# Two casts, two products, a broadcast and a preparation step change places in a two-layer encoder kernel

## The chip, the cores and the metric

The kernel runs on one NeuronCore of a Trainium2 chip. Its time is the device time of one execution in microseconds (us). TensorE (PE in the profile) multiplies matrices, VectorE (DVE), ScalarE (ACT) and GpSimd (POOL) do element work, and SyncE (SP) issues most of the loads. Each engine runs its own queue of instructions in order; an instruction that waits for another engine holds all that stand behind it in its queue.

## The reference

Two sequences, 256 and 512 positions of width 1024, run through the same two layers. A layer is a mixer and a feed-forward part, each behind a normalisation whose scale, shift and gate come from a conditioning vector. Layer 0 mixes with an mLSTM of four heads in both directions, layer 1 with attention in a window of 128 around each position (16 query heads, 4 key heads). Cut to what matters here:

```python
def trunk(x, c, ...):
    for l in range(DEPTH):                                   # 2
        mod = jax.nn.silu(c) @ adaln_w[l] + adaln_b[l]
        sh1, sc1, g1, sh2, sc2, g2 = [...]
        h = rmsnorm(x, norm_g[l, 0]) * (1 + sc1) + sh1
        y = mlstm_mixer(h, ...) if l % N_MIXERS == 0 else swa_mixer(h, ...)
        x = x + g1 * y
        h = rmsnorm(x, norm_g[l, 1]) * (1 + sc2) + sh2
        x = x + g2 * conv_ffn(h, ffn_w_up[l], ffn_conv_w[l], ffn_conv_b[l], ffn_w_down[l])
    return rmsnorm(x, final_g)

def conv_ffn(h, w_up, conv_w, conv_b, w_down):
    u = h @ w_up                                             # 1024 -> 2 * 2816
    u = lax.conv_general_dilated(u, ...) + conv_b            # 3 taps, each channel alone
    g, val = u[..., :D_FF], u[..., D_FF:]
    return (jax.nn.silu(g) * val) @ w_down
```

All is float32.

## The kernel before

The 768 positions lie along the free dimension, the channels on the 128 partitions: `x` is eight blocks (`c` from 0 to 7) of 128 x 768, in slabs of four. A float32 product is made from two rounded parts: ACT casts a weight or a factor to a high part (`whi`, `zh`, `s1h`, L276), DVE subtracts to get the low part (`wlo`, `zl`, `s1l`, L277), and PE adds three matmuls, high by high, low by high and high by low. Weights come in `raw` tiles of 128 x 1024 (512 KB, six buffers, L285), their parts lie in three buffers each.

**Feed-forward.** The up projection is done in 11 parts of 4 channel blocks; a part is two pairs (`i` = 0 and 1), a pair is a two-by-two block product in Strassen's way, with seven products instead of eight. `pair` (L1471) loads two weight tiles, makes sums of their halves (POOL, L1479 to L1491), splits them, and gathers the products in fixed banks of the accumulator memory. L1495 copies rows that are finished into a bank, on which PE then adds (the bank copy); L1500, L1506 and L1519 copy further sums out of or between banks; L1524 and L1525 add two sums into result rows. `s1h` and `s1l` are the parts of one weight sum, for the fifth product. The rows then pass the convolution (`conv`: L1679 on ACT, L1681 and L1682 on DVE, 771 elements), `silu` (L1689, ACT) and `product` (L1695, POOL, gate times value, 128 x 772), whose result is split on ACT and DVE for the down product.

Part 0 of a layer is done otherwise, by `head` (L1550 on): both of its pairs at once, in an order written by hand for PE, ACT and DVE, mixed with the end of the mixer's output projection. `last_tile` is that projection as a generator: each step gives one block's matmuls, and the residual sum L548 on DVE. Behind each block follows its square for the normalisation (L113, ACT) and the sum of squares (L122, DVE), and PE adds the squares up over the partitions (L138). `prepare` makes the weight sums and parts for `head` ahead of time.

**Order elsewhere.** Outside `head`, a scheduler places the instructions from a cost model, and `issue_after` tells it that what follows must not be issued ahead of a named instruction. The code around `pair` uses it to hang `silu` and `product` of an earlier part on two copies (`behind`): L1506 for the gates, L1519 for the split.

**mLSTM.** The heads come one after another. `maxima` broadcasts two rows of running maxima of the next head from memory into a slab (L676, two loads of 384 KB on SP). ACT makes exponentials of them (L768 to L775, tile `E`), from which come the weights `PT`. PE sums `PT` by the values into `pa` banks, ACT scales one bank into the output (L828) and DVE adds the other (L829), which frees the banks.

## Time and profile before

| | |
|---|---|
| median of three runs | 1801.85 us (1797.5 to 1803.8) |
| the profiled execution | 1795.42 us |
| its span | 1793.5 us |
| granted TensorE clock, mean | 0.998 |
| PE, DVE, ACT, POOL busy | 98%, 77%, 50%, 28% |

A profile row of a timeline gives the start in us, the duration, the engine, the line, the operation, and the tiles it writes and reads; in square brackets stands how long the engine idled before it and what released it. Matmuls of 128 x 384 start about 0.17 us apart when nothing is waited for. A row of the waits gives what waited, for what, the sum in us, the count and the longest. A tile's number is left out in the profile and given in the listings of the order below.

### The profile page before, as it was taken

The numbers are of one execution on the slowest core, as the hardware profiler recorded it, in microseconds if no ns is written. First come the engines' busy times: TensorE is split into PE (matmuls) and PEld (weight loads), VectorE is DVE, ScalarE is ACT, GpSimd is POOL, SyncE is SP. The second block draws the span as 40 slices with busy tenths as digits, with TensorE's granted clock in tenths as the row PEclk, the third lists the DMA queues.
The fourth block names the chain that finished last, engine by engine and source line by source line (L and its number), as shares of the span: only waits on it lengthen the run. The fifth ranks groups of instructions, "written<-read, shape, count | busy, mean of one in ns | idle before, by whom it ended". The sixth has DMA issues, their size and how long they took to land.

```text
span 1793.5 us, 28843 instructions
## 1 busy us (share of the span) xinstructions
PE 1763.6 (98%) x11164; PEld 1643.1 (92%) x11164; DVE 1380.5 (77%) x2197; ACT 897.8 (50%) x1806; POOL 506.3 (28%) x425
## 2 busy tenths in 40 slices
PE   9999999999989999999999999999999999999998
PEld 6988888989989999999999998989989999999998
DVE  5797678976897777777778867767897777777777
ACT  4455444543574444444444666664564444444443
POOL 1111011230234333333332123320244333333323
PEclk9999999999999999999999999999999999999999
DMA  9265756554222222222223222142122222222202
GB/s 375 97 196 174 230 199 199 164 181 142 71 71 71 71 68 65 61 66 71 71 71 108 86 80 61 44 146 83 47 71 71 71 71 71 71 71 71 71 24 71
DMA packets 64180, 184.02 MB, mean 103 GB/s; under 512 B 6211, under 2 KB 24291, under 8 KB 63916
## 3 DMA queue, kind: packets, MB, share of 16 engines
q1 hardware_dynamic: 63260, 180.77, 31.5%
q8 instruction: 87, 1.43, 0.3%
q0 software_dynamic: 208, 0.90, 0.1%
q10 hardware_dynamic: 576, 0.52, 0.1%
q14 instruction: 49, 0.40, 0.1%
HBM read 175.73 MB, written 6.44 MB: 102 GB/s over the span
## 4 chain that ended last, share of the span: by engine, by line
PE 87%; DVE 7%; DMA 3%; issue 2%; ACT 2%; SPq 0%; POOL 0%; POOLq 0%; DVEq 0%; ACTq 0%
PE ps L270 27%; PE pa L270 24%; PE ps L1447 11%; PE ps L1448 11%; PE ps L1450 11%; PE pa L1286 1%; DVE junk L488 1%; DMA raw<-in_w_dram 1%; DMA slab<-in_adaln_h_dram 1%; DVE wlo L277 1%; DMA raw<-in_adaln_t_dram 1%; PE pa L1447 1%; PE pa L1448 1%; PE pa L1450 0%; DVE slab L277 0%
## 5 line engine op out<-in xcount | busy, mean ns | idle before, releaser
L276 ACT CAST whi<-raw 128x1024 fp32r<-128x1024 f32 x227 | 238.0, 1050 | 307.8 <-PE pa L270 144.6
L277 DVE TENSOR_TENSOR wlo<-raw,whi 128x1024 fp32r<-128x1024 f32 x227 | 295.0, 1300 | 109.1 <-ACT whi L276 106.7
L270 PE MATMUL pa<-slab,whi 128*128 128x256 f32 (+1 forms) x1280 | 306.9, 335 | 0.0
L270 PEld LDWEIGHTS pa<-slab,whi 128*128 128x128 f32 x1280 | 222.3, 188 | 21.2
L548 DVE SCALAR_TENSOR_TENSOR slab<-pa,mod,slab 128x256 f32<-128x256 f32 (+1 forms) x320 | 188.0, 604 | 67.8 <-PE pa L270 67.7
L270 PE MATMUL pa<-slab,wlo 128*128 128x512 f32 (+1 forms) x640 | 204.7, 333 | 0.0
L270 PE MATMUL ps<-zh,whi 128*128 128x256 f32 (+1 forms) x520 | 179.0, 345 | 0.6 <-ACT whi L276 0.6
L1447 PE MATMUL ps<-zh,whi 128*128 128x384 f32 x504 | 171.5, 340 | 4.8 <-ACT ps L1495 2.4
L270 PE MATMUL ps<-zl,whi 128*128 128x256 f32 (+1 forms) x520 | 174.7, 336 | 0.9 <-DVE zl L513 0.8
L270 PE MATMUL ps<-zh,wlo 128*128 128x256 f32 (+1 forms) x520 | 173.4, 335 | 0.2 <-DVE wlo L277 0.2
L270 PE MATMUL ps<-slab,whi 128*128 128x384 f32 (+2 forms) x704 | 172.1, 330 | 0.9 <-DVE slab L277 0.5
L1448 PE MATMUL ps<-zl,whi 128*128 128x384 f32 x504 | 170.1, 337 | 0.8 <-DVE zl L1404 0.8
L1450 PE MATMUL ps<-zh,wlo 128*128 128x384 f32 x504 | 169.0, 335 | 0.0
L488 DVE CUSTOM_DVE_ANT_0 junk<-raw,crow,cstt 128x1024 bf16<-128x1024 f32 x112 | 148.3, 1324 | 11.1 <-DMA raw<-in_adaln_t_dram 10.4
L1695 POOL TENSOR_TENSOR slab<-slab 128x772 f32<-128x772 f32 x44 | 87.0, 1976 | 239.2 <-DVE slab L1682 239.2
L270 PEld LDWEIGHTS pa<-slab,wlo 128*128 128x128 f32 x640 | 120.5, 188 | 13.2
L1681 DVE SCALAR_TENSOR_TENSOR slab<-slab,cstt,slab 128x771 f32<-128x771 f32 x88 | 111.1, 1265 | 26.3 <-ACT slab L1679 26.3
L1479 POOL TENSOR_TENSOR raw<-raw 128x512 f32<-128x512 f32 x40 | 67.3, 1682 | 212.2 <-DMA raw<-in_w_dram 106.0
L270 PEld LDWEIGHTS ps<-slab,whi 128*128 128x128 f32 x704 | 122.3, 188 | 3.4 <-ACT whi L276 0.9
L1682 DVE SCALAR_TENSOR_TENSOR slab<-slab,cstt,slab 128x771 f32<-128x771 f32 x88 | 113.9, 1294 | 0.8
L270 PE MATMUL ps<-slab,wlo 128*128 128x384 f32 (+2 forms) x352 | 114.2, 327 | 0.1
L270 PEld LDWEIGHTS ps<-zh,whi 128*128 128x128 f32 x520 | 98.3, 189 | 17.0 <-issue 6.4
(327 smaller groups left out, 4292.6 us busy)
## 6 DMA issues: line engine op xcount, KB each, us to landing
raw<-in_w_dram SPq DMA_DIRECT2D x206, 512.0 KB, 3.7
raw<-in_adaln_t_dram SPq DMA_DIRECT2D x56, 512.0 KB, 4.2
raw<-in_adaln_w_dram SPq DMA_DIRECT2D x24, 512.0 KB, 4.4
slab<-in_x_dram SPq DMA_DIRECT2D x12, 512.0 KB, 6.9
slab<-in_adaln_h_dram SPq DMA_DIRECT2D x12, 512.0 KB, 9.3
xs<-slab SPq DMA_DIRECT2D x6, 512.0 KB, 3.4
bt<-brow SPq DMA_DIRECT2D x16, 192.0 KB, 3.3
slab<-xs SPq DMA_DIRECT2D x6, 512.0 KB, 6.0
```

The source lines that it names most:

```text
L270: self.nc.tensor.matmul(out, lhsT, rhs, start=start, stop=stop)
L276: nc.scalar.copy(hi, src)
L277: return nc.vector.tensor_tensor(lo, src, hi.bitcast(F32), ALU.subtract)
L488: nc.vector.tensor_tensor_reduce(out=junk, in0=w, in1=row[:, s], scale=1.0, scalar=self.cst(AB + 48 * l + j), op0=ALU.mult, op1=ALU.add, a ...
L548: return self.nc.vector.scalar_tensor_tensor(x, o, self.mod[l][:, gc + c, q : q + 1], x, ALU.mult, ALU.add)
L1447: mm(o, wh[:, k], hi[k], start=start and k == 0, stop=False, skip_group_check=True)
L1448: mm(o, wh[:, k], lo[k], start=False, stop=False, skip_group_check=True)
L1450: mm(o, wl[:, k], hi[k], start=False, stop=k == 3, skip_group_check=True)
L1479: tt(q[2], q[2], q[3], ALU.add)
L1681: stt(y[:, 1:], u[:, :-1], w(0), y[:, 1:], ALU.mult, ALU.add)
L1682: stt(y[:, :-1], u[:, 1:], w(2), y[:, :-1], ALU.mult, ALU.add)
L1695: nc.gpsimd.tensor_tensor(y, y, yrow[:, j], ALU.mult)
```

## The change

Five edits. All products and sums stay; only engine and order change.

1. In `head`, the cast of `top`, the sum of the second pair, into a spare slab, and the two subtractions behind it, move from before the last projection blocks to behind them.
2. In `pair` of part 1, second pair, the convolutions of the first pair's rows are started behind the bank copy and the `s1l` subtraction, by a new argument `start`, and not ahead of the pair.
3. The products of part 0 (those whose split is held back, `wait`) are made by DVE and not by POOL. There are two per layer.
4. `prepare` may issue only behind the square of the second block of the first half's normalisation (`Norm.second`).
5. The maxima of the next head may issue only behind the last weight load that the head before has issued (`last_load`).

```diff
@@ Norm.square
-        net.nc.scalar.activation(sq, self.x(c), AF.Square)
+        act = net.nc.scalar.activation(sq, self.x(c), AF.Square)
         self.sums.append(sq)
         self.count += 1
+        if self.count == 2:
+            self.second = act.ins
@@ raw
-        self.nc.sync.dma_start(t, src)
+        self.last_load = self.nc.sync.dma_start(t, src)
@@ mLSTM
                 soon = self.slab([P, 4, T])
-                maxima(h + 1, soon)
+                with self.tc.issue_after(self.last_load.ins):
+                    maxima(h + 1, soon)
@@ pair
-        self.fp_copy_split(s1h, s1l, q[2])
+        sub = self.fp_copy_split(s1h, s1l, q[2])
...
-        nc.scalar.copy(b, fork)
+        act = nc.scalar.copy(b, fork)
+        if start:
+            with self.tc.issue_after(act.ins), self.tc.issue_after(sub.ins):
+                start()
@@ head
-        nc.scalar.copy(s1[1][0], top)
         wc[0], low = split(ra[0])
         next(last_tile)
         for t in banks[0][1:]:
             mark(t)
         next(last_tile)
-        tt(s1[1][1], top, s1[1][0].bitcast(F32), ALU.subtract)
-        tt(top, a22, q[1][0], ALU.subtract)
         self.norm.add()
+        low()
         next(last_tile)
         self.norm.begin(1)
         next(last_tile)
-        low()
         for _ in last_tile:
             pass
+        nc.scalar.copy(s1[1][0], top)
+        tt(s1[1][1], top, s1[1][0].bitcast(F32), ALU.subtract)
+        tt(top, a22, q[1][0], ALU.subtract)
@@ ffn
-        early = self.prepare(u0, pool)
+        with self.tc.issue_after(self.behind.second):
+            early = self.prepare(u0, pool)
@@ product
-                nc.gpsimd.tensor_tensor(y, y, yrow[:, j], ALU.mult)
+                (nc.vector if wait else nc.gpsimd).tensor_tensor(y, y, yrow[:, j], ALU.mult)
@@ up
-                for j in range(2):
-                    conv(urow[:, 2 * i + j], yrow[:, 2 * i + j], i * FC + 2 * p + j)
+                def convs(i=i):
+                    for j in range(2):
+                        conv(urow[:, 2 * i + j], yrow[:, 2 * i + j], i * FC + 2 * p + j)
+                start = None
+                if p == 1 and i == 0:
+                    start = convs
+                else:
+                    convs()
```

`self.behind` is the normalisation of the first half behind the mixer. The lines of the new text lie two to eight further down: L1495 becomes L1499, L1519 becomes L1526, L1681 and L1682 become L1689 and L1690, L1695 becomes L1703.

The first place is the end of the projection in layer 0, on ACT. `slab_4988` is the spare slab, `nt_4967`, `nt_5024` and `nt_5058` are squares, `whi_4994` is the high part for `wc[0]`. Before:

```order
L113 ACTIVATE nt_4933<-slab_4394 128x384
L113 ACTIVATE nt_4967<-slab_4394 128x384
L1576 CAST slab_4988<-raw_4696 128x512
L1570 CAST whi_4994<-raw_4690 128x1024
L113 ACTIVATE nt_5024<-slab_4394 128x384
L113 ACTIVATE nt_5058<-slab_4394 128x384
L160 ACTIVATE nr_5072<-pa_5053 128x3
```

With the change, for the same stretch:

```order
L113 ACTIVATE nt_4933<-slab_4394 128x384
L1577 CAST whi_4993<-raw_4690 128x1024
L113 ACTIVATE nt_4967<-slab_4394 128x384
L113 ACTIVATE nt_5023<-slab_4394 128x384
L113 ACTIVATE nt_5056<-slab_4394 128x384
L1595 CAST slab_4988<-raw_4696 128x512
L162 ACTIVATE nr_5072<-pa_5051 128x3
```

The cast into the slab now stands behind both last squares, and the cast of `wc[0]` ahead of three of them.

The second place is the second pair of part 1 in layer 0, on DVE. `slab_5409` holds the convolved rows of part 0 and `slab_5423` those of part 1, `slab_5410` the split product of part 0, `s1l_5788` belongs to the next pair. Before:

```order
L1681 SCALAR_TENSOR_TENSOR slab_5409<-slab_4982,cstt,slab_5409 128x771
L1682 SCALAR_TENSOR_TENSOR slab_5409<-slab_4982,cstt,slab_5409 128x771
L277 TENSOR_TENSOR wlo_5542<-raw_5531,whi_5541 128x1024
L1681 SCALAR_TENSOR_TENSOR slab_5409<-slab_4982,cstt,slab_5409 128x771
L1682 SCALAR_TENSOR_TENSOR slab_5409<-slab_4982,cstt,slab_5409 128x771
L1524 TENSOR_TENSOR slab_4983<-ps_4387,nt_5446 128x384
L277 TENSOR_TENSOR wlo_5546<-raw_5529,whi_5545 128x1024
L1525 TENSOR_TENSOR slab_4983<-ps_4386,nt_5489 128x384
L277 TENSOR_TENSOR slab_5410<-slab_5409,slab_5410 128x772
L1681 SCALAR_TENSOR_TENSOR slab_5423<-slab_4983,cstt,slab_5423 128x771
L277 TENSOR_TENSOR s1l_5788<-raw_5776,s1h_5787 128x512
```

With the change:

```order
L1689 SCALAR_TENSOR_TENSOR slab_5409<-slab_4982,cstt,slab_5409 128x771
L1703 TENSOR_TENSOR slab_5409<-slab_5409 128x772
L1690 SCALAR_TENSOR_TENSOR slab_5409<-slab_4982,cstt,slab_5409 128x771
L279 TENSOR_TENSOR wlo_5536<-raw_5525,whi_5535 128x1024
L1689 SCALAR_TENSOR_TENSOR slab_5409<-slab_4982,cstt,slab_5409 128x771
L1531 TENSOR_TENSOR slab_4983<-ps_4387,nt_5446 128x384
L279 TENSOR_TENSOR wlo_5540<-raw_5523,whi_5539 128x1024
L1690 SCALAR_TENSOR_TENSOR slab_5409<-slab_4982,cstt,slab_5409 128x771
L1532 TENSOR_TENSOR slab_4983<-ps_4386,nt_5489 128x384
L279 TENSOR_TENSOR slab_5410<-slab_5409,slab_5410 128x772
L279 TENSOR_TENSOR s1l_5788<-raw_5776,s1h_5787 128x512
L1703 TENSOR_TENSOR slab_5409<-slab_5409 128x772
```

One product (L1703) comes in ahead of `s1l_5788` and one behind it, the convolution of `slab_5423` leaves its place ahead of it, and L1531 stands ahead of a convolution step. On ACT the bank copy now stands ahead of the convolution's own step (L1687), which before stood ahead of it, and the cast `whi_5539` ahead of the second `silu`.

The third place is head 2 of the mLSTM, on ACT. `slab_2807` is the slab of head 3's maxima, `slab_1932` that of head 2, which takes its output. Before:

```order
L823 ACTIVATE dn_2838<-pa_2847 128x1
L828 ACTIVATE slab_1932<-pa_2813,dn_2812 128x256
L831 ACTIVATE nt_2836,ss_2811<-slab_1932 128x256
L828 ACTIVATE slab_1932<-pa_2839,dn_2838 128x256
L831 ACTIVATE nt_2862,ss_2811<-slab_1932 128x256
```

With the change:

```order
L827 ACTIVATE dn_2838<-pa_2847 128x1
L778 ACTIVATE E_3306<-slab_2807,aT 128x384
L832 ACTIVATE slab_1932<-pa_2813,dn_2812 128x256
L774 ACTIVATE E_3306<-E_3306,aT 128x128
L771 ACTIVATE E_3325<-slab_2807,aT 128x128
L778 ACTIVATE E_3325<-slab_2807,aT 128x256
L773 ACTIVATE E_3306<-E_3306,aT 128x128
L835 ACTIVATE nt_2836,ss_2811<-slab_1932 128x256
L832 ACTIVATE slab_1932<-pa_2839,dn_2838 128x256
```

The exponentials of head 3, which stood 19 rows ahead of the first L828, are now mixed with the scaling of head 2's output. On SP the two broadcast loads move from between the weight loads `raw_2562` and `raw_2568` to behind `raw_2803`, past twelve loads.

More of the change, by code (lines that the diff above doesn't have):

```diff
@@ L568, in out_proj @@
         self.norm = norms[1]
+        self.behind = norms[0]
         self.turn = 1
@@ L1469, in outset, with pair @@
         self.evict(r1, o)
-    def pair(self, pool, u, bank, rows, rest=False, behind=None):
+    def pair(self, pool, u, bank, rows, rest=False, behind=None, start=None):
         nc = self.nc
@@ L1719, in up @@
                         bank = lambda j: self.pa()[:, :H] if j == 1 and other else fixed(j)
-                        self.pair(pool, u0 + 3 * p + i, bank, rows, p == 1, held.pop() if held else None)
-                for j in range(2):
-                    conv(urow[:, 2 * i + j], yrow[:, 2 * i + j], i * FC + 2 * p + j)
+                        self.pair(pool, u0 + 3 * p + i, bank, rows, p == 1, held.pop() if held else None, start)
+                def convs(i=i):
+                    for j in range(2):
+                        conv(urow[:, 2 * i + j], yrow[:, 2 * i + j], i * FC + 2 * p + j)
+                start = None
+                if p == 1 and i == 0:
+                    start = convs
+                else:
+                    convs()
                 if i == 0:
```

## The prediction

> **What bounds the kernel now.** I read the page first, then the waits of the TensorE queue, and then the timelines of the engines round the longest of those waits.
>
> ```profile
> span 1793.5 us, 28843 instructions
> PE 1763.6 (98%) x11164; PEld 1643.1 (92%) x11164; DVE 1380.5 (77%) x2197; ACT 897.8 (50%) x1806; POOL 506.3 (28%) x425
> ```
>
> TensorE (PE) is busy for 98% of the span, and no other engine for more than 77%: PE's matmuls, end to end, are the time. The change touches no matmul, so only PE's idle time, about 30 us, can move. The waits say where it is; each row gives the waiting PE group, what released it, the sum, the count and the longest:
>
> ```profile
> PE ps L1450 <- DVE s1l L277: 3.8, 2, 1.9
> PE pa L138 <- DVE nt L122: 3.4, 2, 1.7
> PE ps L1447 <- ACT ps L1495: 2.4, 2, 1.2
> PE ps L1447 <- ACT nt L1519: 2.0, 2, 1.0
> PE pa L1286 <- ACT pt L1290: 1.5, 2, 0.9
> PE pa L270 <- DVE slab L277: 0.2, 1, 0.2
> ```
>
> The four largest waits come twice each, once per layer, and all four (11.6 us) lie in the code that the change rewrites. The order of instructions on PE itself is otherwise kept. So the question is how much of some 13 us each edit frees, and what is late next.
>
> **Edit 1, the early cast in head(), once per layer.** Layer 0, at the end of the projection, in the timelines of ACT, DVE and PE:
>
> ```profile
> 469.81 0.62 ACT L1576 CAST slab<-raw 128x512 fp32r<-128x512 f32 x1 [5.13 <-PE ps L270]
> 471.28 0.52 ACT L113 ACTIVATE nt<-slab 128x384 f32<-128x384 f32 x1
> 466.30 0.62 DVE L548 SCALAR_TENSOR_TENSOR slab<-ps,mod,slab 128x384 f32<-128x384 f32 x1 [1.03 <-PE ps L270]
> 471.83 0.56 DVE L122 TENSOR_TENSOR nt<-nt,nt 128x384 f32<-128x384 f32 x1
> 470.49 0.34 PE L270 MATMUL ps<-slab,wlo 128*128 128x384 f32 x1
> 472.54 0.80 PE L138 MATMUL pa<-inv,nt 128*128 128x2 f32 x6 [1.71 <-DVE nt L122]
> ```
>
> ACT sat 5.13 us on the cast L1576, whose target is a slab that the projection's last tiles still read. Behind it stood the square L113 of a row block that DVE had finished at 466.92. The square ran at 471.28, its sum L122 ended at 472.39, and PE started at 472.54, although its last projection matmul had started at 470.49. Two neighbouring matmuls of this shape start 0.18 apart, so PE lost 2.05 - 0.18 = 1.87 us.
>
> After the change the square stands ahead of that cast and needs only the 466.92. Even behind the cast of wc[0] (1.05, as every ACT cast of 128x1024 whose row is quoted below) it ends by 468.5, and the sum by 469.1, before PE's own 470.66. So this wait goes whole. What is late next is the second half's last square, after the last tile: its residual, square and sum (0.6 + 0.5 + 0.6) follow 470.7, so it is done at about 472.4, when the first sums have run on PE and the next products can cover it. The moved cast and the two subtractions now stand behind the tile loop. They feed only the second pair's fifth product, which PE reaches after four starting products of the layer, and that lead hides them; without it they cost 1.4 (two subtractions of 128x512, 0.68 each as in s1l's row below). I take 1.85 per layer, **3.7**. The bounds per layer are 1.87, and -0.2 if the second sum shows whole (0.65) and the lead is gone (1.4).
>
> **Edits 2 and 3, the second pair of part 1, once per layer.** Three PE waits follow one another here, the last at the fifth product of the next pair. The rows of DVE, POOL and ACT in layer 0:
>
> ```profile
> 517.13 1.22 DVE L277 TENSOR_TENSOR wlo<-raw,whi 128x1024 fp32r<-128x1024 f32 x1
> 518.87 2.06 DVE L1681 SCALAR_TENSOR_TENSOR slab<-slab,cstt,slab 128x771 f32<-128x771 f32 x1
> 520.97 2.51 DVE L1682 SCALAR_TENSOR_TENSOR slab<-slab,cstt,slab 128x771 f32<-128x771 f32 x1
> 523.40 2.32 DVE L277 TENSOR_TENSOR wlo<-raw,whi 128x1024 fp32r<-128x1024 f32 x1
> 525.64 1.01 DVE L1681 SCALAR_TENSOR_TENSOR slab<-slab,cstt,slab 128x771 f32<-128x771 f32 x1
> 526.69 1.02 DVE L1682 SCALAR_TENSOR_TENSOR slab<-slab,cstt,slab 128x771 f32<-128x771 f32 x1
> 527.63 0.55 DVE L1524 TENSOR_TENSOR slab<-ps,nt 128x384 f32<-128x384 f32 x1
> 528.09 2.67 DVE L277 TENSOR_TENSOR wlo<-raw,whi 128x1024 fp32r<-128x1024 f32 x1
> 530.69 0.54 DVE L1525 TENSOR_TENSOR slab<-ps,nt 128x384 f32<-128x384 f32 x1
> 531.16 1.59 DVE L277 TENSOR_TENSOR slab<-slab,slab 128x772 fp32r<-128x772 f32 x1
> 532.67 1.01 DVE L1681 SCALAR_TENSOR_TENSOR slab<-slab,cstt,slab 128x771 f32<-128x771 f32 x1
> 533.60 0.68 DVE L277 TENSOR_TENSOR s1l<-raw,s1h 128x512 fp32r<-128x512 f32 x1
> 534.20 0.95 DVE L277 TENSOR_TENSOR slab<-slab,slab 128x772 fp32r<-128x772 f32 x1
> 517.24 2.88 POOL L1479 TENSOR_TENSOR raw<-raw 128x512 f32<-128x512 f32 x1 [4.10 <-DVE slab L1682]
> 520.08 2.58 POOL L1695 TENSOR_TENSOR slab<-slab 128x772 f32<-128x772 f32 x1
> 522.62 2.02 POOL L1491 TENSOR_TENSOR raw<-raw,raw 128x512 f32<-128x512 f32 x1
> 527.86 1.83 POOL L1695 TENSOR_TENSOR slab<-slab 128x772 f32<-128x772 f32 x1 [3.22 <-DVE slab L1682]
> 529.64 2.28 POOL L1479 TENSOR_TENSOR raw<-raw 128x512 f32<-128x512 f32 x1
> 525.62 0.47 ACT L1519 COPY nt<-ps 128x384 f32<-128x384 f32 x1
> 529.21 0.47 ACT L1495 COPY ps<-slab 128x384 f32<-128x384 f32 x1
> ```
>
> The first wait: the copy L1519 stands behind a weight cast that came late because POOL did a product (L1695, 2.58) ahead of the subtraction L1491. The second: the bank copy L1495 stands behind a convolution on ACT and, through bank 4387, behind DVE's L1524. The third: s1l, done at 534.28, stands at the end of a DVE queue in which whatever overlaps a POOL row is stretched (1.01 to 2.51, 1.22 to 2.67).
>
> Since PE's matmuls do not depend on which wait came when, the gain here is how much earlier s1l ends, up to the 4.1 us that the three waits hold (1.0 + 1.2 + 1.9). From 518.87 to s1l, DVE's unstretched work before is 1.01 + 1.02 + 1.22 + 1.01 + 1.02 + 0.55 + 1.22 + 0.54 + 0.95 + 1.01 + 0.68 = 10.2 us; it took 15.4, so 5.2 us are stretch, beside 10.0 us of POOL rows inside that window (11.59 less the 1.63 before 518.87). After, DVE gains one product (0.95, the nearest row being the 128x772 subtraction of two slabs) and loses the first L1681 of the moved convolutions (1.01): 10.2 again. POOL keeps the tail of L1479 (1.25), L1491 (2.02) and the next L1479 (2.28): 5.6 us, so at the same share 2.9 us of stretch. Then s1l ends at 518.87 + 10.2 + 2.9 = 532.0, which is 2.3 earlier; if POOL's last row comes after s1l (its load is released by a wlo subtraction) it is 1.2 more, 3.5. I take 2.7 per layer, **5.4** for both. The other inputs are in time: the copy L1519 follows a cast that can now start when L1491 ends, near 522.2, and the bank copy follows L1524, near 526.2, with PE due at 527.1. So waits one and two all but go, and about 1.5 to 2 us stay at the third.
>
> [...]
>
> The bounds: the low one has every operation as long as its longest row: 2.06 + 1.59 + 2.51 + 2.67 + 2.06 + 0.55 + 2.67 + 2.51 + 0.54 + 1.59 + 0.68 = 19.4, s1l at 538.3, a loss of 4.0 per layer. The high one is the gain of 4.1.
>
> The convolutions that move behind the bank copy feed part 1's own gates, due a pair later. DVE's second product, behind s1l now, feeds the second half of part 0's down products, which PE takes up only behind the rest of that fifth product and the first half. I cost both at nothing; were that lead gone, it would be one more product, 0.95 per layer.
>
> **Edit 4, prepare() held back.** Only in layer 1 does work move: casts and subtractions for the first Strassen pair leave the attention tail.
>
> ```profile
> 1178.41 1.05 ACT L276 CAST zh<-raw 128x1024 fp32r<-128x1024 f32 x1 [2.33 <-DMA raw<-in_w_dram]
> 1179.37 0.36 ACT L1290 COPY pt<-pa 128x256 f32<-128x256 f32 x1
> 1208.31 0.69 DVE L1546 TENSOR_TENSOR raw<-raw 128x512 f32<-128x512 f32 x1 [1.77 <-DMA raw<-in_w_dram]
> ```
>
> ACT's copy L1290, for which PE waits (1.5 us in two waits above), ran right behind such a cast, which had stood on a load; without it the copy can start up to 0.96 us earlier, more than the longest of the two waits. I take **1.3** of the 1.5, bounds 0 and 1.5. The casts and subtractions land in the output projection; on DVE they are 1.22 + 1.22 + 1.36 = 3.8 us, and DVE idled 1.77 us there ahead of 1208.31. The other 2.0 us are covered by the lead that the weight splits have on PE; without that cover they are the price.
>
> **Edit 5, the maxima.** The two broadcast loads for head 3 move behind the last weight load on SP's queue.
>
> ```profile
> DMA to landing us min/median/max: 4.5/6.8/8.1
> 249.46 2.40 SPq L285 DMA_DIRECT2D raw<-in_w_dram  x2
> 260.65 3.79 PE L270 MATMUL pa<-slab,PT 128*128 128x258 f32 x30
> ```
>
> The gain is the 0.2 us at the last of the waits above, since a weight no longer loads beside them. The price: they are issued at about 251.9 and land near 258.7, at worst 260.0; ACT now reads them ahead of L828, which frees the banks that PE wants at 260.65. At 258.7 plus a 0.6 us exponential it still fits; at 260.0 it costs about 0.5, and 1.0 when the second bank slips too. I take **0.2**, bounds -1.0 and 0.2.
>
> **The sum.** 3.7 + 5.4 + 1.3 + 0.2 = 10.6 us. The span of 1793.5 becomes 1782.9. The profiled execution took 1795.4 against a median of 1801.85 of the runs shown, which differ among themselves from 1797.5 to 1803.8; taken off that median the sum gives 1791.2, and I say **1791**.
>
> **Rivals.** *DVE takes back the pair.* The product goes to the engine that already ends last there (DVE s1l is the largest wait), so s1l could stay at 534.3. Then 3.7 + 1.3 + 0.2 = 5.2 is left: 1796.6. For it speaks DVE's unstretched work, which does not shrink; against it the 5 us of stretch and the POOL rows that leave.
>
> *Slower: the DVE queue overflows.* If the added product waits on POOL as L1682 did, and all behind it as in the low bound, s1l ends 4.0 later per layer: 8.0 - 5.2 = 2.8 us slower, 1804.7. It decides once s1l ends after about 536.9, 2.6 us later than now. Against it: two of POOL's four later rows leave the window.
>
> *Waits only move.* PE reaches the next place early and waits there: the second half's sum after edit 1 and the third wait of edits 2 and 3 take all but a few us, and the output projection pays its 2.0: of the 10.6 us, 5.4 and 1.3 stay away and 2.0 are paid, so 1.9 are gained, 1800.0. For it speaks that ACT and DVE follow PE closely in all these places; against it DVE's idle time right after head's wait.
>
> **Chances.** The forecast 0.64, the first rival 0.18, moved waits 0.11, slower 0.07. A measurement of this kernel tells about 0.3% (5.4 us) from no change, so faster is below 1796.4, slower above 1807.3. The forecast gives 0.64 to faster, and the first rival, which ends beside the bound, half of its own and moved waits a little: 0.75. The rest of these two and a part of the last, whose 2.8 us lie within the bound, are the same: 0.20. That leaves 0.05 for slower. All bounds together run from 1788 (3.7 + 8.2 + 1.5 + 0.2 = 13.6 gained) to 1813 (0.4 + 8.0 + 2.0 + 1.0 = 11.4 lost); they will not all fall on one side. The range reaches over the first rival and most of moved waits, and below 1788 by 2.5 us for the scatter of medians: 1785.5 to 1800.
>
> **What would show it.** Edit 1: no PE wait at L138 above 0.3, ACT's slab cast behind both squares. Edits 2 and 3: the PE waits on the copies L1495 and L1519 (L1499 and L1526 in the new text) under 0.4 each, s1l still a wait of 1.5 to 2, L1703 on DVE at about 1 us. Edit 4: the pt wait under 0.4. Edit 5: no PE wait on slab L832. The prediction is wrong if s1l ends later than before relative to the pair's first matmul, or if new PE waits above 1 us stand in the output projection or at 260.

## The result, and the profile after

The changed kernel takes 1787.5 us, median of four runs (1784.4 to 1788.9), against 1802.4 of the kernel before (1797.5 to 1803.8): a ratio of 0.992, with a 95% interval of 0.9896 to 0.9943. A second comparison, told below, gave 0.9928 (0.9912 to 0.9944). That is faster by more than 0.3%, inside the range, and 3.5 us below the 1791 of the forecast. The profiled execution took 1784.4 us with a span of 1782.3, where the sum had led to 1782.9. Two of the runs below (edits 1 and 3 undone) had one slow execution among ten, 1963 and 4442 us, and their medians and ratios leave it out, as the ratios do for one of the kernel before.

The page's first rows after:

```profile
span 1782.3 us, 28844 instructions
PE 1761.7 (99%) x11164; PEld 1643.4 (92%) x11164; DVE 1377.7 (77%) x2201; ACT 896.2 (50%) x1806; POOL 494.9 (28%) x421
```

PE's idle time fell from 29.9 to 20.6 us, which is 9.3 of the span's 11.2. The waits of the TensorE queue (waiting group, what released it, sum, count, longest) tell where; these are the rows of the changed places and behind them that are left above 0.2 us, and the row of the scaled output, slab L832, that the prediction names:

```profile
PE ps L1454 <- DVE s1l L279: 2.1, 2, 1.6
PE ps L1451 <- ACT ps L1513: 1.4, 2, 0.7
PE pa L272 <- DVE slab L550: 0.8, 1, 0.8
PE pa L272 <- ACT slab L832: 0.4, 1, 0.4
```

Five of the six waits that the prediction started from have no row any more: the norm's sum (3.4), the bank copy (2.4), the copy nt (2.0), pt (1.5) and the weight's low part (0.2). The wait for s1l, the sixth, shrank from 3.8 to 2.1. That for the scaled output, slab L832 (L828 before), is what it was, 0.4; it stands at 179 us, in an earlier head than the one whose loads moved. Two have grown or are new: the copy L1513, at 0.3 in the kernel before (there L1506), and slab L550, which had none at this place.

**The head.** Layer 0 after the change, timelines of ACT, DVE and PE (start, duration, then in brackets the idle time before and what ended it):

```profile
466.05 0.53 ACT L113 ACTIVATE nt<-slab 128x384 f32<-128x384 f32 x1 [3.58 <-DVE slab L550]
470.62 0.53 ACT L113 ACTIVATE nt<-slab 128x384 f32<-128x384 f32 x1 [4.05 <-DVE slab L550]
471.06 0.60 ACT L1595 CAST slab<-raw 128x512 fp32r<-128x512 f32 x1
466.61 0.56 DVE L124 TENSOR_TENSOR nt<-nt,nt 128x384 f32<-128x384 f32 x1 [0.59 <-ACT nt L113]
469.60 0.34 PE L272 MATMUL ps<-slab,wlo 128*128 128x384 f32 x1
469.77 0.72 PE L140 MATMUL pa<-inv,nt 128*128 128x2 f32 x6
471.84 0.72 PE L140 MATMUL pa<-inv,nt 128*128 128x2 f32 x6
```

The square now waits for its row block alone, its sum L124 ends at 467.17, and PE starts the sums at 469.77, 0.17 after its last projection matmul: no gap. The cast that stood ahead of it runs at 471.06, behind both squares, and the second sums at 471.84 have no wait either.

**The pair.** The second pair of part 1 in layer 0, timelines of DVE and POOL:

```profile
516.03 2.06 DVE L1689 SCALAR_TENSOR_TENSOR slab<-slab,cstt,slab 128x771 f32<-128x771 f32 x1
518.01 2.06 DVE L1703 TENSOR_TENSOR slab<-slab 128x772 f32<-128x772 f32 x1
519.99 1.01 DVE L1690 SCALAR_TENSOR_TENSOR slab<-slab,cstt,slab 128x771 f32<-128x771 f32 x1
520.92 1.21 DVE L279 TENSOR_TENSOR wlo<-raw,whi 128x1024 fp32r<-128x1024 f32 x1
525.99 1.99 DVE L279 TENSOR_TENSOR slab<-slab,slab 128x772 fp32r<-128x772 f32 x1
527.89 0.68 DVE L279 TENSOR_TENSOR s1l<-raw,s1h 128x512 fp32r<-128x512 f32 x1
528.50 0.95 DVE L1703 TENSOR_TENSOR slab<-slab 128x772 f32<-128x772 f32 x1
514.68 2.58 POOL L1483 TENSOR_TENSOR raw<-raw 128x512 f32<-128x512 f32 x1 [4.39 <-DMA raw<-in_w_dram]
517.23 2.01 POOL L1495 TENSOR_TENSOR raw<-raw,raw 128x512 f32<-128x512 f32 x1
525.85 1.29 POOL L1483 TENSOR_TENSOR raw<-raw 128x512 f32<-128x512 f32 x1 [6.61 <-DMA raw<-in_w_dram]
```

From the start of L1689 to the end of s1l it is now 528.57 - 516.03 = 12.5 us; before it was 15.4. In layer 1, and in both layers of a second profile of this kernel (below), it is 11.5. Three DVE rows are still about twice their own length, and each overlaps a POOL row. L1690 and the wlo subtraction, which were 2.51 and 2.32 long beside POOL's work, run undisturbed at 1.01 and 1.21.

**What is late next.** Some 30 us on, in the first pair of part 2, timelines of ACT and PE:

```profile
559.61 1.05 ACT L278 CAST whi<-raw 128x1024 fp32r<-128x1024 f32 x1 [4.39 <-PE pa L272]
560.56 0.47 ACT L1513 COPY ps<-ps 128x384 f32<-128x384 f32 x1
561.09 0.44 PE L1451 MATMUL ps<-zh,whi 128*128 128x384 f32 x1 [0.71 <-ACT ps L1513]
```

The cast of the pair's third weight needs the buffer of a weight that PE reads in its last down product. It starts when that product has been read, and the copy L1513, whose bank PE wants, stands behind it. In the order of the kernel before, PE had seven matmuls between that down product and the one that needs the copy; in the new order four. Three starts of 0.17 are 0.5 us less cover, and the two waits grew from 0.15 to 0.7 each.

The other new wait is in layer 1, in the down products behind the pair, timelines of PE and DVE:

```profile
1338.89 0.51 PE L272 MATMUL pa<-slab,whi 128*128 128x256 f32 x2 [0.78 <-DVE slab L550]
1337.21 0.96 DVE L279 TENSOR_TENSOR slab<-slab,slab 128x772 fp32r<-128x772 f32 x1 [1.96 <-ACT slab L278]
```

DVE stood 1.96 us for a split of ACT that itself hangs on part 1's product on POOL. In exchange PE's wait for s1l in this layer is only 0.5. In layer 0 it is the other way round: 1.6 at s1l, none at L550. What differs is which of two rows is held: in layer 0 POOL's weight sum L1483 took 1.29 and DVE's subtraction from 525.99 took 1.99 (rows above), and in layer 1 the subtraction, from 1307.96, took its own 0.95, and the sum

```profile
1308.19 3.35 POOL L1483 TENSOR_TENSOR raw<-raw 128x512 f32<-128x512 f32 x1 [6.97 <-DVE slab L1532]
```

### The profile page after: what moved, and what is told of

Same layout as the page of the kernel before. It is cut to its first block, busy times and chain, and to the rows that moved or that the text cites. A ratio compares the mean times of both kernels' runs of the same rounds, so it can differ in the third digit from the quotient of the medians.

```text
span 1782.3 us, 28844 instructions
## 1 busy us (share of the span) xinstructions
PE 1761.7 (99%) x11164; PEld 1643.4 (92%) x11164; DVE 1377.7 (77%) x2201; ACT 896.2 (50%) x1806; POOL 494.9 (28%) x421
## 4 chain that ended last, share of the span: by engine, by line
PE 84%; DVE 9%; DMA 2%; ACT 2%; issue 2%; POOL 0%; SPq 0%; DVEq 0%; ACTq 0%
PE ps L272 28%; PE pa L272 22%; PE ps L1451 10%; PE ps L1452 10%; PE ps L1454 10%; PE pa L1290 1%; DVE slab L1689 1%; DMA raw<-in_w_dram 1%; DVE wlo L279 1%; DMA slab<-in_adaln_h_dram 1%; DVE junk L490 1%; DVE slab L1690 1%; DVE slab L550 1%; DVE slab L279 1%; ACT whi L278 0%
## 5 line engine op out<-in xcount | busy, mean ns | idle before, releaser
L279 DVE TENSOR_TENSOR wlo<-raw,whi 128x1024 fp32r<-128x1024 f32 x227 | 289.0, 1274 | 110.2 <-ACT whi L278 109.3
L550 DVE SCALAR_TENSOR_TENSOR slab<-pa,mod,slab 128x256 f32<-128x256 f32 (+1 forms) x320 | 187.5, 603 | 66.9 <-PE pa L272 66.9
L1703 POOL TENSOR_TENSOR slab<-slab 128x772 f32<-128x772 f32 x40 | 78.1, 1953 | 228.8 <-DVE slab L1690 228.8
L1689 DVE SCALAR_TENSOR_TENSOR slab<-slab,cstt,slab 128x771 f32<-128x771 f32 x88 | 112.4, 1280 | 26.0 <-ACT slab L1687 26.0
L1483 POOL TENSOR_TENSOR raw<-raw 128x512 f32<-128x512 f32 x40 | 66.0, 1653 | 228.4 <-DMA raw<-in_w_dram 124.2
L1690 DVE SCALAR_TENSOR_TENSOR slab<-slab,cstt,slab 128x771 f32<-128x771 f32 x88 | 110.9, 1260 | 0.7
```

Source lines behind the costliest of these rows:

```text
L279: return nc.vector.tensor_tensor(lo, src, hi.bitcast(F32), ALU.subtract)
L550: return self.nc.vector.scalar_tensor_tensor(x, o, self.mod[l][:, gc + c, q : q + 1], x, ALU.mult, ALU.add)
L1483: tt(q[2], q[2], q[3], ALU.add)
L1689: stt(y[:, 1:], u[:, :-1], w(0), y[:, 1:], ALU.mult, ALU.add)
L1690: stt(y[:, :-1], u[:, 1:], w(2), y[:, :-1], ALU.mult, ALU.add)
L1703: (nc.vector if wait else nc.gpsimd).tensor_tensor(y, y, yrow[:, j], ALU.mult)
```

## The experiments

Beside medians I use one number that comes from the timeline of PE: the time from the start of its 301st matmul to the start of its last (*body*), and in layer 1 from the 7201st to the 9001st (*stage*, which holds the tail of the attention, the output projection, the head and the pair). The body leaves out the program's first 40 us, which differ between executions (last section). Before has a body of 1746.5 us and a stage of 290.7, the changed kernel 1734.9 and 284.3. Ratios are to runs of the kernel before on the same chip, with 95% intervals. A single undone edit is worth less than about 0.3%, so for these the verdict rests on waits and body.

**u1_cast_early: edit 1 undone.**

```diff
+        nc.scalar.copy(s1[1][0], top)
         wc[0], low = split(ra[0])
...
+        tt(s1[1][1], top, s1[1][0].bitcast(F32), ALU.subtract)
+        tt(top, a22, q[1][0], ALU.subtract)
         self.norm.add()
-        low()
...
+        low()
         for _ in last_tile:
             pass
-        nc.scalar.copy(s1[1][0], top)
-        tt(s1[1][1], top, s1[1][0].bitcast(F32), ALU.subtract)
-        tt(top, a22, q[1][0], ALU.subtract)
```

> The changed kernel with edit 1 undone in both layers (early cast again ahead of the last projection blocks), all else as changed. My theory (the cast holds the squares back on ScalarE, and nothing later gives the gain back): the two PE waits of 1.7 on the sum of squares return, the span rises from 1782.3 by 3.7 to about 1786.0, and the pair of part 1 is unchanged relative to its first matmul. Rival (waits only move: what edit 1 frees is paid at the next place where VectorE is late): the span rises by less than 1.5, and the waits behind the head shrink by the rest.

Measured: 1791.5 us, ratio 0.9956 (0.9934 to 0.9978). PE's waits have the old row back, at its old size:

```profile
PE pa L140 <- DVE nt L124: 3.4, 2, 1.7
```

The body is 1739.0, 4.1 above the changed kernel and 3.2 above its second profile (below); the stage is 2.0 longer. Edit 1 is worth what was forecast, 3.7, within that scatter, and nothing behind it takes it back.

**u3_products_pool: edit 3 undone** (part 0's products on POOL again, the convolutions still behind the bank copy).

```diff
-                (nc.vector if wait else nc.gpsimd).tensor_tensor(y, y, yrow[:, j], ALU.mult)
+                nc.gpsimd.tensor_tensor(y, y, yrow[:, j], ALU.mult)
```

> The changed kernel with edit 3 undone: part 0's products are made by GpSimd again, the convolutions still start behind the bank copy. My theory (the gain in the pair comes from GpSimd's rows leaving VectorE alone): the time from VectorE's first step behind s1l to the end of the next s1l is about 15.4 us again and not 12.5; the first and third PE wait return (1.0 and 1.9 per layer), the second, on the bank copy, stays away or shows at the third place; the span rises by 3 to 6. Rival (the bank copy ahead of the convolution carries the gain): the span rises by less than 1.5.

Measured: 1793.2 us, ratio 0.996 (0.9939 to 0.998), body 1742.2. Waits of PE, then the first and last row of DVE's stretch in layer 0:

```profile
PE ps L1454 <- DVE s1l L279: 4.7, 2, 2.4
PE ps L1451 <- ACT ps L1499: 0.5, 2, 0.2
```

```profile
520.09 2.05 DVE L1689 SCALAR_TENSOR_TENSOR slab<-slab,cstt,slab 128x771 f32<-128x771 f32 x1
534.83 0.68 DVE L279 TENSOR_TENSOR s1l<-raw,s1h 128x512 fp32r<-128x512 f32 x1
```

DVE's stretch is 15.4 us long, as in the kernel before. The bank copy's wait did fall, from 2.4 to 0.5, and the wait for s1l rose by 0.9 in its stead. The body is 7.3 above the changed kernel, more than the 3 to 6 expected of the span; part of that is the clock, told at the next run.

**u23_pair_before: edits 2 and 3 undone**, the edit above and this:

```diff
-                if p == 1 and i == 0:
+                if False:
                     start = convs
```

> The changed kernel with edits 2 and 3 undone, so that the pair of part 1 is as before. My theory: all three waits return (1.0, 1.2 and 1.9 per layer), and the waits that are new behind the pair (0.7 on the copy between banks twice, 0.8 on a block sum in layer 1) go; the span rises by 4 to 6. Against the run with only edit 3 undone it tells what edit 2 does alone: by my theory nothing at the third wait, since s1l ends the VectorE queue at the same time, so the two spans agree within 0.5. Rival: the second wait is worth its own 1.2 per layer, and this one is 2.4 longer.

Measured: 1791.1 us, ratio 0.9948 (0.9927 to 0.9969), body 1743.3. PE's waits in the pair are those of the kernel before to a tenth:

```profile
PE ps L1454 <- DVE s1l L279: 3.8, 2, 1.9
PE ps L1451 <- ACT ps L1499: 2.4, 2, 1.2
PE ps L1451 <- ACT nt L1526: 2.0, 2, 1.0
```

From the start of the matmul ahead of the first wait to that of the matmul that s1l releases, PE takes 9.54 us in layer 0 here and 9.57 in the run before, which has edit 2 without edit 3. Edit 2 by itself is thus worth nothing: it only moves the wait from the copy to s1l. The body is 8.4 above the changed kernel, over the 4 to 6 expected of the span. From the 3401st to the 3701st matmul, which hold the pair and the copy behind it, PE takes 59.3 us here, 57.7 in the kernel before with the same waits, and 55.9 in the changed kernel; in layer 1, from the 8381st to the 8681st, 59.3, 57.8 and 55.8. So of 3.5 us per layer 1.9 to 2.0 are waits, and some 1.6 come from the clock, which behind these waits was 0.83 over 10 us, in both layers of this run and of the one before, against 1.00 in the kernel before's first profile (last section).

**u2_convs_ahead: edit 2 undone, edit 3 kept** (the second diff alone).

> The changed kernel with edit 2 alone undone. Its instructions come out in the same order on all engines as with it, only the numbers of some buffers differ. Theory: with the products on VectorE the scheduler puts the bank copy ahead of the convolution anyway, so edit 2 does nothing: span 1782.3 within 1, the pair's rows the same within 0.1 us. Rival (a buffer that changes places changes a wait): another span by more than 1.5.

Measured: 1785.2 us, ratio 0.9908 (0.9877 to 0.9939), which overlaps the changed kernel's; body 1736.5, stage 284.3 as in the changed kernel. No wait on the bank copy comes back:

```profile
PE ps L1454 <- DVE s1l L279: 3.0, 2, 1.6
```

Once the products are on DVE, the convolutions come behind the bank copy in any case. The gain in the pair is edit 3's, and what is left at s1l (here 1.4 and 1.6, and nothing at L550), and the 1.4 at L1513, are there without edit 2.

**u4_prepare_free: edit 4 undone.**

```diff
-        with self.tc.issue_after(self.behind.second):
-            early = self.prepare(u0, pool)
+        early = self.prepare(u0, pool)
```

> The changed kernel with edit 4 undone: the first casts of the next weights may run in the attention tail again. My theory: the two PE waits on the copy of the transposed weights return (1.5 in sum, 1.9 with the start of the matmuls behind them), and the output projection is no faster for it: span up by 1.5 to 2.3 from 1782.3. Rival (the moved work is paid in the output projection): span within 0.7.

Measured: 1787.7 us, ratio 0.9935 (0.9918 to 0.9952). The old wait is back:

```profile
PE pa L1290 <- ACT pt L1294: 1.3, 2, 0.7
```

The stage is 286.3, 2.0 longer. These 2.0 us are all lost by the second of the two waits, ahead of the output projection. From there (the 7690th matmul) to the stage's end PE takes 227.3 us with edit 4 and without it, so the output projection pays nothing for the casts and subtractions that moved into it. Edit 4 is worth about 2 us in the trace, too little to show in medians.

**u5_maxima_early: edit 5 undone.**

```diff
-                with self.tc.issue_after(self.last_load.ins):
-                    maxima(h + 1, soon)
+                maxima(h + 1, soon)
```

> The changed kernel with edit 5 undone: the broadcast of the next head's maxima is issued early again, beside a weight load. My theory: the wait of 0.2 to 0.4 at the score products of the next head returns and the wait on the scaled output some 35 us later goes; both are small, and the span stays within 0.6 of 1782.3. Rival (the late broadcast costs at ScalarE's queue head): without it the span falls by 1 or more.

Measured: 1788.0 us, ratio 0.9936 (0.9919 to 0.9953), body 1736.5. A wait for a weight's low part returns:

```profile
PE pa L272 <- DVE slab L279: 1.1, 1, 1.1
```

It was 0.2 and 0.6 in the two profiles of the kernel before. With edit 5 it is gone in nine of eleven profiles, and 0.2 and 0.4, four matmuls on, in the other two (edit 2 undone, and v1 below). The row on the scaled output, 0.4, stands in every profile, far ahead of the moved loads, so it does not go as expected and tells nothing of them. From 235 to 300 us, where the late loads could cost, PE's waits have no row, with edit 5 or without it. In time edit 5 does not show: 1788.0 us and a body of 1736.5 lie beside the changed kernel's 1787.7 and 1735.8 below.

**v1_sum_on_vector: one POOL row moved.** To see whether the rest of the wait at s1l is POOL's doing, the weight sum of the next pair's second half runs on DVE behind s1l.

```diff
+        if ease:
+            with self.tc.issue_after(self.sub.ins):
+                nc.vector.tensor_tensor(q[2], q[2], q[3], ALU.add)
+        else:
+            tt(q[2], q[2], q[3], ALU.add)
-        tt(q[2], q[2], q[3], ALU.add)
...
+        self.pair(..., start, p == 2 and i == 1)
```

> The changed kernel with one more GpSimd operation moved: the first weight sum of the second pair of part 2 (128x512) goes to VectorE, behind the s1l subtraction. In the profile of the change that sum runs on GpSimd at 525.85 to 527.14 and VectorE's subtraction beside it takes 1.99 and not 0.95. If two such operations exclude each other (theory), that subtraction falls to about 0.95 and s1l ends 1.0 earlier in layer 0; the third wait falls from 1.6 to about 0.6 there, and the span by 1 to 2. Rival (VectorE is the bound there, one more operation on it costs its own 0.68): no gain, the third wait stays above 1.2.

Measured: 1783.2 us, ratio 0.991 (0.9892 to 0.9928), body 1732.8, stage 282.7. DVE's timeline in layer 0:

```profile
526.45 0.94 DVE L279 TENSOR_TENSOR slab<-slab,slab 128x772 fp32r<-128x772 f32 x1
527.32 0.68 DVE L279 TENSOR_TENSOR s1l<-raw,s1h 128x512 fp32r<-128x512 f32 x1
```

The subtraction of 1.99 us is 0.94 without the POOL row beside it. PE's waits at s1l fall to 1.0 in sum, and there is none on slab L550:

```profile
PE ps L1454 <- DVE s1l L279: 1.0, 2, 0.5
PE ps L1451 <- ACT ps L1517: 1.1, 2, 0.5
```

What is left is the copy (here L1517).

**v3_all_products_vector: all products on DVE.**

```diff
-                (nc.vector if wait else nc.gpsimd).tensor_tensor(y, y, yrow[:, j], ALU.mult)
+                nc.vector.tensor_tensor(y, y, yrow[:, j], ALU.mult)
```

> The changed kernel with the products of all eleven parts on VectorE. Theory (GpSimd's products cost VectorE more by holding it than they would on VectorE itself): VectorE's busy time rises by less than the 36 products' own 0.95 each (34 us), since its other rows beside GpSimd get shorter; PE's waits in the up and down parts do not grow by more than 2 in all, span within 3 of 1782.3. Rival (VectorE becomes the bound once it carries all products): PE's waits on VectorE grow by 5 or more and the span with them.

Measured: 1796.5 us, ratio 0.9982 (0.997 to 0.9993), body 1744.3, 9.4 above the changed kernel. 40 products moved (the expectation had 36). The products' group (count, busy time, mean ns) and PE's largest wait:

```profile
L1703 DVE TENSOR_TENSOR slab<-slab 128x772 f32<-128x772 f32 x44 | 45.5, 1034 | 0.6
```

```profile
PE ps L1451 <- ACT ps L1513: 9.8, 14, 0.7
```

Two things follow. DVE's busy time rose from 1377.7 to 1395.2 only, 17.5 us for 40 products that last 0.95 each, or 38: the rest came back as stretch that is gone. By groups, the rows of L1690, wlo and s1l are 31 us shorter in sum, those of L1689 13 us longer. And the loss is not DVE as a bound: it is the copy L1513, which now stands behind a late cast in 14 places instead of two, 8.4 us more. In all 14 the row ahead of it on ACT is a weight cast that waited for PE. What in the new order brings this about stays open.

**again_changed: the changed kernel once more**.

> The changed kernel itself once more, as the comparison for the two kernels beside it. Expected: 0.8% faster than before, PE waits as in its first profile, with the third wait of the pair and the block-sum wait behind it trading about 1 us in each layer (1.7 and 0.2, or 0.7 and 1.0).

Measured: 1787.7 us, ratio 0.9928 (0.9912 to 0.9944), body 1735.8, stage 284.3.

```profile
PE pa L272 <- DVE slab L550: 1.6, 2, 0.8
PE ps L1454 <- DVE s1l L279: 1.0, 2, 0.5
```

Here both layers have 0.5 at s1l and 0.8 at L550, as layer 1 had in the first profile. The two waits trade places, as POOL's weight sum or DVE's subtraction is the one that is held. In the twelve places of six profiles (the two of this kernel, and those with edits 1, 2, 4 and 5 undone) either the subtraction takes 1.9 to 2.0 us and PE waits 1.4 to 1.6 at s1l and not at L550, or POOL's sum takes 3.3 to 3.7 and PE waits 0.5 at s1l and 0.8 at L550. In the profiles of this kernel it makes no difference to PE: from the 3401st to the 3701st matmul it takes 55.9 us in the one case and 55.8 in the other. The copy's wait is 1.4 again.

**v12_sum_and_cast: v1, and the pair's third weight cast behind the copy.** This takes away what the copy L1513 stood behind.

```diff
-        wb = self.split(rb)
+        if not late_b:
+            wb = self.split(rb)
...
         fork = nc.scalar.copy(d, b)
+        if late_b:
+            with self.tc.issue_after(fork.ins):
+                wb = self.split(rb)
```

> The changed kernel with the weight sum of part 2's second pair on VectorE (as in the run before), and in part 2's first pair the cast of the third weight behind the copy between two banks instead of ahead of it. Theory for the wait of 0.7 per layer on that copy: the copy stands on ScalarE behind a cast that must wait for PE's last down product; ahead of the cast, the copy runs when its bank is full, and PE's next quarter needs only the copy. Expected: the wait falls from 0.7 to about 0.2 per layer, so with the sum moved PE waits fall by about 3.5 us against the changed kernel, and it is 0.2% faster than it. Rival (PE then waits for the cast instead): the wait only changes its name, and no more than the sum's own 2.8 us is gained.

Measured: 1781.8 us, ratio 0.9899 (0.9881 to 0.9916), body 1731.0, stage 282.1. No row of PE waits for the copy any more. It runs here as soon as PE has written its source, in ACT's timeline at

```profile
560.94 0.46 ACT L1518 COPY ps<-ps 128x384 f32<-128x384 f32 x1 [4.42 <-PE ps L1454]
```

So the cast ahead of it had been the cause. All of PE's waits together are 11.1 us, 3.3 to 3.7 less than in the two profiles of the changed kernel, as expected.

**v6_no_pool_beside: v12, and two more of POOL's operations on DVE**, the weight sum of part 2's first pair and the last subtraction of part 1's second pair.

```diff
-            tt(q[2], q[2], q[3], ALU.add)
+            (nc.vector.tensor_tensor if first else tt)(q[2], q[2], q[3], ALU.add)
...
-        tt(q[2], q[3], q[0], ALU.subtract)
+        (nc.vector.tensor_tensor if last else tt)(q[2], q[3], q[0], ALU.subtract)
```

> The same, and the two other GpSimd operations beside this stretch (the weight sum of part 2's first pair, the last subtraction of part 1's second pair) on VectorE too. Theory (an operation on GpSimd holds VectorE's row beside it for its whole length): the rows of 2.05 (a convolution step and the product) fall to about 1.0, VectorE's stretch up to s1l gets 0.8 shorter although it carries two operations of 0.68 more, and the third wait of the pair goes from 0.5 to under 0.2. Rival (VectorE's own work counts): the stretch gets longer by 1.4 less what the rows give, and the third wait grows to 1 or more.

Measured: 1781.0 us, ratio 0.9888 (0.9867 to 0.9909), body 1730.2, stage 281.8. DVE's timeline, and PE's largest wait:

```profile
516.89 1.00 DVE L1697 SCALAR_TENSOR_TENSOR slab<-slab,cstt,slab 128x771 f32<-128x771 f32 x1
517.82 0.95 DVE L1711 TENSOR_TENSOR slab<-slab 128x772 f32<-128x772 f32 x1
```

```profile
PE ps L1451 <- ACT ps L1518: 1.1, 2, 0.6
```

The two rows of 2.06 are 1.00 and 0.95, DVE's stretch up to s1l is 9.95 us instead of 11.5, and the wait at s1l is gone. A wait on the copy is back, 0.55 per layer, for another reason: no cast stands ahead of the copy, which runs as soon as PE has written its bank, but in this order PE has no matmul left to do meanwhile. This run has the lowest median: 6.7 us below the changed kernel on the same chip, with intervals that do not meet; it is not told apart from v12.

**before_again: the kernel before once more.**

> The kernel before once more, for a second profile of it. In the two runs with the pair as before the granted TensorE clock falls to 0.83 in the 10 us behind the three waits, in both layers, and costs about 1.8 us each time; in the first profile of the kernel before it stays at 1.00 with the same waits. Theory (the waits close together can lower the clock, not in every execution): this profile shows 0.83 behind the pair in at least one layer, and its span less the slow start is above 1752. Rival (only the order with edit 1 in it does so): 1.00 again in both layers.

Measured: 1799.6 us, ratio 0.9991 (0.997 to 1.0012), with the same waits in the changed places. Its body is 1752.6, though, 6.1 longer than in the first profile of the same kernel. As expected, the clock falls behind the pair's waits, to 0.83 over 10 us in layer 0, while in layer 1 it stays at 1.00; the last section shows where the 6.1 us lie.

## Why the prediction was right, and where it was off

**Edit 1: right.** "So this wait goes whole", 3.7: the wait went from 3.4 to none, and undoing it costs 3.2 to 4.1. The second sums, named as late next, were covered as argued, and the moved cast was never waited for.

**Edits 2 and 3: the mechanism right, the size off.** The sum put s1l's end 2.3 earlier, or 3.5 if POOL's last row came after it. It came 15.4 - 12.5 = 2.9 earlier in layer 0, where POOL's last row came before it, and 3.9 earlier in layer 1. So the mechanism was right and the gain at s1l somewhat larger than the sum had it: the sum counted 2.28 us for POOL's last row, which took 1.29 in layer 0 and held nothing up in layer 1. Waits one and two went as said. Counted as waits, the pair's 8.2 us became 2.1, a gain of 6.1. The step that failed is the cost behind the pair: "I cost both at nothing" spoke of the convolutions and of the second product, and indeed neither is waited for, but the new order had other prices. The copy L1513 lost three matmuls of cover (1.1 more in two layers), and slab L550 came late in one layer (0.8). So 6.1 - 1.1 - 0.8 = 4.2 were kept, not 5.4; by the starts of PE's matmuls over pair and copy (u23 above) it is 1.9 + 2.0 = 3.9. The prediction followed the queues of DVE, POOL and ACT in the pair, and said that PE's order was "otherwise kept"; three matmuls moved there, and these were the ones that mattered. The two prices are removable: with the weight sum and the cast moved (v12) the body falls by another 4 to 5 us.

Crediting both edits together hid that one of them does nothing. Edit 2 alone moves a wait (9.58 against 9.55 us), and edit 3 alone already has the gain.

"L1703 on DVE at about 1 us" held for the second product (0.95), not for the first (2.06), which ran beside POOL's L1495.

**On the stretch** the rows read as if DVE's were held until the POOL row beside it ended, which fits better than the share of the sum (5.2 us of stretch beside 10.0 of POOL rows). L1703 from 518.01, held until POOL's 519.24 and then 0.95 long, would end at 520.19, and by the share at 519.6; it ended at 520.07. The subtraction from 525.99, held until 527.14, would end at 528.09, and by the share at 527.5; it ended at 527.98. And with the POOL rows away the same rows last 0.94 to 1.00 (v1, v6). Not every row is held, though: in the kernel before, L1525 took 0.54 in the middle of a POOL row. What decides it no run shows.

**Edit 4: right, a little small.** The wait of 1.5 went whole, not 1.3 of it, and undoing edit 4 lengthens the stage by 2.0, for 1.3 of waits: PE's starts fall back by 0.8 and 0.9 us at the two waits, and by 0.2 in between. The output projection does not pay.

**Edit 5: right in sign.** Undone, it costs a wait of 1.1 in that profile rather than 0.2, and nothing that shows in the time. "No PE wait on slab L832" was a poor test: the row of 0.4 is in both kernels (L828 before), at another head.

**The rivals.** *DVE takes back the pair* fell: s1l comes 2.9 or 3.9 earlier. *Slower* fell with it. *Waits only move* holds for about 2 of the pair's 6 us, and for nothing else.

**The sum.** By places: 3.7 + 4.2 + 2.0 + 0.2 = 10.1, against 10.6 forecast and 11.2 in the spans. The rest of the span's gain is scatter of waits that the change does not touch; E at L780, for one, is 0.8 here, 1.4 before, and 1.2 in the changed kernel's second profile. That the medians differ by 14 to 15 us, more than the profiled executions do, no edit's wait explains; the clock does. For the ten runs of the changed kernel and 66 of the kernel before, span and mean granted clock are on record. At 0.998 the median span is 1793.8 us before (11 runs) and 1782.8 changed (2 runs), at 0.997 it is 1795.5 (12) and 1785.7 (4), at 0.996 it is 1797.2 (12) and 1787.1 (3): 10 to 11 us apart at the same clock, which is what the sum gives (the clock is recorded to 0.001, or some 2 us). The other 3 to 4 us come from the mix of clocks: 31 of the 66 have 0.995 or less, and none of the ten. The forecast did not have that; it is part of why 1787.5 came out below 1791.

## What to carry to other kernels

When two engines' operations are longer beside each other (here a subtraction on DVE 1.99 us and not 0.95, a weight sum on POOL 3.35 and not 1.29), moving a short operation from the slower to the faster one (a product takes 1.98 us on POOL on average, in the kernel before, and 0.95 on DVE undisturbed) can cost the faster far less than its length (40 products of 0.95 us cost 17.5 us of DVE's time, not 38), but moving all of them changes the order elsewhere and can cost more than it frees (a body 9.4 us longer). When a wait goes, look for copies behind it that stand after a cast which needs a buffer, and count the matmuls that cover them in the new order as well as in the old. Of two edits aimed at the same wait, undo each alone: one of them may be doing nothing.

## What the runs showed of the hardware

**The clock at the start of a program differs between executions.** The view by stretches, with the granted clock third from last, first of the changed kernel and then of its second profile:

```profile
0.00:20.00 20.00, 17.44 (x143) 15.13 (x144) 9.76 (x30) 9.67 (x24) 3.55 (x8) 1.00 0.92 340
```

```profile
0.00:20.00 20.00, 17.45 (x123) 14.70 (x123) 8.33 (x24) 8.88 (x22) 3.56 (x8) 0.93 0.92 338
20.00:40.00 20.00, 19.95 (x145) 13.03 (x145) 10.83 (x24) 6.37 (x10) 0.00 (x0) 0.90 1.04 405
```

In the second the granted clock is 0.93 and 0.90 in these stretches, 20 x 0.07 + 20 x 0.10 = 3.4 us of full clock less, and PE reaches its 301st matmul 3.8 us later after its first. That stays to the end: the spans of 1782.3 and 1786.8 differ by it, and the bodies by 0.9. So a span alone does not compare two kernels to a few us. What goes with it is a wait of PE just before, at 14 us, which is 0.8 in the first and 1.3 in the second:

```profile
PE pa L272 <- DVE nt L938: 0.8, 1, 0.8
```

```profile
PE pa L272 <- DVE nt L938: 1.3, 1, 1.3
```

In eight of the fourteen profiles this wait is 1.2 to 1.3 us, and in these eight the clock of the first 20 us is 0.89 to 0.93; in the six others it is 0.5 to 0.8, and the clock 1.00. That the wait is the cause is not shown by a run that takes it away.

**The clock falls after short waits of PE too, in some executions.** The same view of PE in the second profile of the kernel before, behind the head's wait of 1.7 us and behind the pair's three waits, then of the run with edits 2 and 3 undone:

```profile
470.00:480.00 10.00, 8.29 (x46) 0.88 0.13 37
480.00:490.00 10.00, 10.00 (x49) 0.78 0.22 70
540.00:550.00 10.00, 9.08 (x41) 0.83 0.21 63
```

```profile
530.00:540.00 10.00, 8.12 (x35) 0.83 0.34 106
```

Behind the pair, in the second profile of the kernel before, two neighbouring matmuls of 128x384 start at 542.69 and 543.01, 0.32 us apart; up to 542.41 it was 0.17. Worked out from the stretches, 1.2 + 2.2 = 3.4 us of full clock are missing behind the head of layer 0, and 1.7 behind the pair, in the one run as in the other. The first profile of the kernel before, with the same waits, shows 1.00 there, and both profiles of the changed kernel show 1.00 from 300 to 1770 us. In layer 0, from PE's 2251st matmul to its 3501st, the two profiles of the kernel before take 218.9 and 223.6 us, 4.7 apart; in layer 1, where the second has 0.97 and 0.85 from 1260 to 1280 us, behind the head, and 1.00 behind the pair, the stages are 290.7 and 292.1. So the clock fell behind a wait of 1.7, with some 0.7 us of two-column matmuls after it, or behind three of 1.0 to 1.9 within some 10 us, though not each time. Of the 19 runs with edit 3, or 2 and 3, undone, so with the pair's waits back, nine have a mean clock of 0.995 or less, and none of the ten of the changed kernel. So a wait removed can be worth more than its row says: per layer, with edits 2 and 3 undone, some 1.6 us on top of the 1.9 to 2.0 of the waits.
